# Hybrid attention and recurrence block: when the first recurrent half's heads are turned for the output projection, and which instruction the third weight's casts stand behind at a border

## The chip, the cores and the metric

The kernel runs on one core of a Trainium2 chip. Its time is device microseconds of one execution; the figure for a kernel is the median of its runs. One execution was also recorded by the hardware profiler. TensorE (PE) does matmuls and transposes, VectorE (DVE) and ScalarE (ACT) do elementwise work and empty PE's output banks, GpSimd (POOL) and SyncE (SP) issue most of the transfers. Each engine has its own queue and works through it in order.

## The reference, cut to what matters

One layer, 512 tokens, width 2048, all in float32:

```python
h = rms_norm(x, norm1_w) * (1 + scale1) + shift1      # shift, scale, gate: silu(c) @ w_ada + b_ada
aq, ak, av, gq, gf, gi, gg = split(h @ w_in)          # 7 groups of 1024 columns
attn = rms_norm(dilated_attention(rope(norm(aq)), rope(norm(ak)), av))   # 8 heads of 128
ho = hgrn2(gq, gf, gi, lb)                            # 8 heads of 128, causal gated recurrence
hg = rms_norm(ho) * silu(gg)                          # the norm is over each head's 128
x = x + gate1 * (concat([attn, hg]) @ w_out)
x = x + gate2 * (square(relu(h2 @ w_ff1)) @ w_ff2)    # h2: second norm of x with scale2, shift2
```

## The kernel before

Every float32 matmul is three: an operand is split in a rounded part (hi) and the rest (lo), and PE adds hi*hi, hi*lo and lo*hi in one bank (L205 to L207 where the tokens are on the partitions, L213 to L215 where the channels are). ACT makes a rounded part by a cast, DVE the rest by a subtraction: L39 and L40 for a weight (whi, wlo), L246 and L247 for an operand of 128 channels x 512 tokens (hi, lo).

**Projections.** `project` computes 512 columns from the 16 channel blocks k = 0 to 15 into four banks named prj; a weight here is the 128x512 piece for one k, and two of them come with one load (wraw). One weight costs PE 12 matmuls, three for each bank. The projections with this form come in the order: input of the recurrence (gi), attention's aq, ak, av, all for the first half of the heads; then gq, gi, aq, ak, av for the second half; then the gate hg_gate of the first half and of the second. Behind these comes the output projection in four quarters (`project_out`), which has the same form and takes as operands the 16 turned and scaled head blocks (mix): four heads of the first recurrent half, eight of attention, four of the second recurrent half, in that order. All use the same four banks, so the first weight of a projection can only go into a bank that the copies behind the projection before have emptied: L414 in `evac` (gi, av, and by a helper of qk also aq and ak), L572 in `hgrn_q` (gq), L716 in `hg_gate` (gg). "Border" means the place between two projections.

**Background work on PE.** Attention and recurrence are generators in a list, `tasks`. Behind each weight's matmuls `project` calls `tick`, which takes the first generator one `yield` further, so between two weights stands a step of attention or recurrence. In the first output quarter `tick` goes two steps for each of the first ten weights, and more steps are taken there as long as the next operand has not been turned. The PE order is exactly that in which the Python code issues. ACT, DVE and POOL have their instructions ordered by a scheduler's own estimate of times, in which `tc.high_priority()` and `tc.issue_after(x)` (not ahead of instruction x) are what the code can say.

**Casts at a border.** `load_w(..., cast_behind=True)` ties the two casts of a load, and their low parts, behind the instruction that the list `evacuated` holds, if it holds one. `project` asks for it at its third and fourth weight (k0 == 2), and so does the first output quarter. Before the change only `hg_gate` writes to `evacuated`, at each of its four copies, so the list holds its last bank copy: the tie is there at the border between the two gate projections and at the one into the output projection.

**The recurrent half's output.** `hrs` holds each head's norm factors, `gs` the gate of silu form as four token tiles. `hg_out` multiplies, for each of its four heads, the head's output by norm factor and gate, four DVE instructions in place in gs (L731), yields, and turns the head: `to_mix`, four transposes into one bank (L555, ptm) and ACT's scaled copy into mix (L557). It is preceded in `tasks` by attention's norm and followed by `attention_out`, which turns attention's heads one per step. While the second gate projection runs, `split_early` splits turned heads (L246, L247) that exist by k >= 8; what has not been split then is split in the first output quarter. Of the recurrence itself the prediction names these: `forget` (L564, DVE), levels of the chunk product, for which DVE makes an operand z (L611, L612) and the running products Sx, f (L618, L619), the masks (L656, L659), PE's cross products of level 128 (L673, pD), and the weighted sums L132 (acc) of `gemv`, DVE work for the conditioning vectors that runs beside them.

Of the kernel before, what the change touches and what calls it, by code (L numbers as in the profile page):

```python
# [22 lines left out]
DH = 128  # L23
# [21 lines left out]
def hybrid_block(ctx, tc, x, c, positions, norm1_w, w_ada, b_ada, w_in, q_norm_w, k_norm_w,  # L45
# [3 lines left out]
    pe, dve, act, pool = nc.tensor, nc.vector, nc.scalar, nc.gpsimd  # L49
# [18 lines left out]
    def bank(name, tag="bg"):  # L68
        return ps.tile([P, 512], F32, name=name, tag=tag)
# [30 lines left out]
    n2c, aoc, hgc, posc = cols[:, 0:16], cols[:, 16:24], cols[:, 40:41], cols[:, 44:48]  # L100
# [88 lines left out]
    evacuated = []  # L189
# [45 lines left out]
    def slot(name, dt=F32):  # L235
        return io.tile([P, 512], dt, name=name, tag="io")
# [44 lines left out]
    for q in range(4):  # L281
# [5 lines left out]
        for j in range(4):  # L287
# [3 lines left out]
            t = slot("xnT")  # L291
# [71 lines left out]
    def tick(n=1):  # L363

        for _ in range(n):
            while tasks:
                try:
                    next(tasks[0])
                    break
                except StopIteration:  # L370
                    tasks.pop(0)
# [3 lines left out]
    def project(c0, mm, rate=1.85, after=None):  # L375

        banks = [bank("prj", tag="mm") for _ in range(4)]
        for k0 in range(0, NK, 2):
            for j, (whi, wlo) in enumerate(load_w(win_v, k0, c0, 512, None, behind=len(marks) > 2, cast_behind=k0 == 2)):
                k = k0 + j  # L380
                mm(banks, hhi[k], hlo[k], whi, wlo, k == 0, k == NK - 1)
                tick()
                owed[0] += rate
                while owed[0] >= 1.0:
                    bg_step()
                    owed[0] -= 1.0
                if after:
                    after(k)
            marks.append(asked[0])
        return banks  # L390
# [18 lines left out]
    def evac(banks, name):  # L409
        ts = []  # L410
        for ti in range(NT):
            t = slot(name)
            with tc.high_priority():
                act.copy(t, banks[ti])  # L414
            ts.append(t)
        return ts

# [28 lines left out]
    def qk(c0, name, i):  # L446
        ts = evac(project(c0, tok_mm), name)
        rs = sm.tile([P, NT, 4], F32, name=f"rs{i}", bufs=2)
        bgw.insert(0, qk_norm(ts, i, rs))
        return ts if i else (ts, rs)  # L450
# [101 lines left out]
    def to_mix(k, src, hs, wcol):  # L552
        pt = bank("ptm")
        for ti in range(NT):
            pe.transpose(pt[:, ti * P:(ti + 1) * P], src[ti][:, hs], ident)  # L555
        mix[k] = slot("mix")
        act.activation(mix[k], pt, AF.Identity, scale=wcol)  # L557
# [8 lines left out]
    def hgrn_q(ht):  # L566
        qb = project(3072 + ht * 512, ch_mm)
        qs = []
        for h in range(4):
            q = slot("gq")  # L570
            with tc.high_priority():
                act.copy(q, qb[h])  # L572
            qs.append(q)
        for q in qs:
            sg = wk.tile([P, 512], F32, name="sg", tag="ev", bufs=2)
            act.activation(sg, q, AF.Tanh, scale=0.5)
            dve.tensor_scalar(sg, sg, 0.5 * QS, 0.5 * QS, op0=ALU.mult, op1=ALU.add)
            dve.tensor_tensor(q, q, sg, op=ALU.mult)
        return qs
# [130 lines left out]
    def hg_gate(ht):  # L710
        gb = project(6144 + ht * 512, tok_mm, after=split_early if ht else None)
        gs = []
        for ti in range(NT):
            g = slot("gg")
            with tc.high_priority():
                evacuated[:] = [act.copy(g, gb[ti])]  # L716
            gs.append(g)
        for g in gs:
            sg = wk.tile([P, 512], F32, name="sg", tag="ev", bufs=2)
            act.activation(sg, g, AF.Tanh, scale=0.5)  # L720
            dve.tensor_scalar(sg, sg, 0.5, 0.5, op0=ALU.mult, op1=ALU.add)
            dve.tensor_tensor(g, g, sg, op=ALU.mult)
        return gs

    def hg_out(ht, gs, os_, rs):
        for _ in range(3):
            yield
        for h in range(4):
            hs = slice(h * DH, (h + 1) * DH)
            for ti in range(NT):  # L730
                dve.scalar_tensor_tensor(gs[ti][:, hs], os_[h][:, ti * P:(ti + 1) * P], rs[:, h, ti:ti + 1],  # L731
                                         gs[ti][:, hs], op0=ALU.mult, op1=ALU.mult)
            yield
            to_mix(8 + ht * 4 + h, gs, hs, hgc)

    for b in range(4):
        bgw.append(shift_gen(b))
# [125 lines left out]
    v0 = evac(project(2048, tok_mm), "av")  # L863
    tasks.append(attention(q0, k0_, v0))
    hq1 = hgrn_q(1)
    hv1 = evac(project(5120 + 512, tok_mm), "gi")
    tasks.append(hgrn(f1, hq1, hv1, hrs[1]))
# [4 lines left out]
    gs = hg_gate(0)  # L872
    tasks.append(attention_norm((q0[0], q1[0])))
    tasks.append(hg_out(0, gs, f0, hrs[0]))
    tasks.append(attention_out((q0[0], q1[0])))
    gs = hg_gate(1)
    tasks.append(hg_out(1, gs, f1, hrs[1]))
    while bgw:
        bg_step()


    def project_out(q, rate, after):
        banks = [bank("prj", tag="bg" if q % 2 and i < 2 else "mm") for i in range(4)]
        for i0 in range(0, NK, 2):
            for j, (whi, wlo) in enumerate(load_w(wout_v, korder[i0], q * 512, cast_behind=q == 0 and i0 == 2)):
                i = i0 + j
                while q == 0 and len(mixp) <= i:
                    if not split_mix():
                        tick()
                while q == 0 and split_mix():  # L890
                    pass
                tok_mm(banks, *mixp[i], whi, wlo, i == 0, i == NK - 1)
                tick(2 if q == 0 and i < 10 else 1)
                owed[0] += rate
                while owed[0] >= 1.0:
                    bg_step()
                    owed[0] -= 1.0
                after(i)
        return banks
# [4 lines left out]
    banks = project_out(0, 0, nothing)  # L904
# [52 lines left out]
    for q in range(4):  # L957
        xin = []
        for ti in range(NT):
            t = xr.tile([P, 512], F32, name="xin", tag="x")  # L960
            act.dma_start(t, x_t[:, ti, q * 512:(q + 1) * 512])
            xin.append(t)
        if q:
            banks = project_out(q, 1.7, u_split if q == 3 else nothing)
# [223 lines left out]
    def product(i, src, c, ws, tag, by_tile, nxt):  # L1188


        banks = [bank("f2", tag=tag) for _ in range(2)]
        fh, fl = operand(src, c, i)
        ahead = []

        def mm(u, whi, wlo, ts_):
            for a in range(2):
                for t in ts_:
                    ts = slice(t * P, (t + 1) * P)
                    first, end = u + a == 0, u + a == KG
                    pe.matmul(banks[t], lhsT=fh[u][a][:, ts], rhs=whi[:, a], start=first, stop=False)  # L1200
                    pe.matmul(banks[t], lhsT=fh[u][a][:, ts], rhs=wlo[:, a], start=False, stop=False)  # L1201
                    pe.matmul(banks[t], lhsT=fl[u][a][:, ts], rhs=whi[:, a], start=False, stop=end)  # L1202

        if by_tile:
            for t in range(2):
                for u in range(KG):
                    mm(u, *ws[u], (t,))
        else:
            for u in range(KG):
                mm(u, *ws[u], range(2))  # L1210
                if u == KG - 1 or src is hparts:
                    tick()
                if nxt and u < KG - 1:
                    ahead.append(nxt(u))
        return banks, ahead
# [8 lines left out]
    def turn(b, n, cs):  # L1224

        fs = pools["fs2"].tile([P, FORMS, 2, 256], F32, name="fs2")
        for j in (0, 2, 1, 3):
            pt = bank("pt3")
            for ti in range(NT):
                pe.transpose(pt[:, ti * P:(ti + 1) * P], cs[((5, 7), (6, 1))[ti // 2][1 - n]][ti % 2][:, j * P:(j + 1) * P],  # L1230
                             ident)
            act.activation(block(fs, j), halves(pt), AF.Relu)
            if j >= 2:
                v = fs[:, (j - 2) * 2:(j - 2) * 2 + 2]
                act.activation(v, v, AF.Square)
        yield
        yield from make_forms(fs, fparts, 2 * b + n, stage, True, loads if 2 * b + n == NG - 2 else None)
# [21 lines left out]
    def turned(*a):  # L1259
        tasks.append(turn(*a))  # L1260
        while len(tasks) > 1:
            tick()
        tick()
# [82 lines left out]
    for item, following in zip(items, items[1:] + [None]):  # L1346
# [14 lines left out]
        if stage_ == 1:  # L1361
            banks, ahead = product(i, hparts, 0, ws, "bg" if first and j < 2 else "mm", False, call)
# [10 lines left out]
        else:  # L1373
            q, c = blk
            banks, ahead = product(i, fparts, c, ws, "mm", i == 2 and c == NC - 1, call)
# [68 lines left out]
```

## Time and profile before

| | us |
|---|---|
| median of three runs | 2265.33 |
| lowest, highest | 2263.37, 2268.85 |
| the profiled execution, its own time | 2268.35 |
| its span on the core | 2266.6 |
| PE busy in the span | 2211.3 (98%) |
| DVE busy | 1807.2 (80%) |
| ACT busy | 1098.2 (48%) |

The span is the time between first and last record on the core; the execution's own time has what lies around it as well. A row of the timeline gives the start in us from the span's beginning, the busy time, engine, line, operation, the tile that is written and the tiles that are read, shapes, and how many instructions stand in a row (x4); where the engine was idle ahead of the row, brackets give for how long and which instruction released it. A row of the table of stretches gives its window and length, then busy us and instructions of PE, PE's weight loads, DVE, ACT and POOL, the granted clock, the busy share of the DMA engines and GB/s. Matmul ends are modelled, so starts are the better guide on PE. In the list of waits an entry has the sum, the count and the longest.

### The profile page before, as it was taken

To read this page: it belongs to the slowest core of one execution; us is meant where nothing else is said; L and a number is where in the kernel's file an instruction comes from. 1 tells how busy PE (TensorE), PEld (TensorE's weight loads), DVE (VectorE), ACT (ScalarE), POOL (GpSimd) and SP (SyncE) were. 2 spreads that over 40 slices of the span, in tenths; PEclk is the share of its full clock that TensorE was granted. 3 is DMA by queue.
4 is the path that set the end of the run, shared out by engine and by line. 5 is a ranking of instruction groups with operands and counts; after the bars stand their busy time and mean duration, and the time that the engine had idled before them with its cause. 6 is when DMAs were issued, how large, how long until landed. Compare 5 with 4: busy or idle time off the path is not lost.

```text
span 2266.6 us, 33052 instructions
## 1 busy us (share of the span) xinstructions
PE 2211.3 (98%) x11769; PEld 1827.6 (81%) x11769; DVE 1807.2 (80%) x2765; ACT 1098.2 (48%) x1950; POOL 439.5 (19%) x664
## 2 busy tenths in 40 slices
PE   4899999999999999999999999999999999999999
PEld 3788888888888778888887888888888888888887
DVE  6998988678977457778658988988897779967878
ACT  5555444434444454457544565565564333443332
POOL 1000022001210000003232323332232222222221
PEclk9999999999999999999999999999999999999999
DMA  9797655556564248847879789889979987998884
GB/s 327 252 330 260 214 178 167 178 177 205 174 204 145 76 134 280 273 121 263 324 278 350 285 311 387 302 302 364 336 284 372 364 313 260 349 347 312 300 298 166
DMA packets 262581, 598.30 MB, mean 264 GB/s; under 512 B 23220, under 2 KB 43968, under 8 KB 262416
## 3 DMA queue, kind: packets, MB, share of 16 engines
q1 hardware_dynamic: 186800, 332.54, 43.0%
q0 software_dynamic: 70720, 254.21, 30.6%
q10 hardware_dynamic: 4896, 9.44, 1.3%
q8 instruction: 93, 1.52, 0.3%
q14 instruction: 72, 0.59, 0.1%
HBM read 518.49 MB, written 77.61 MB: 263 GB/s over the span
## 4 chain that ended last, share of the span: by engine, by line
PE 73%; issue 10%; DMA 7%; DVE 5%; POOL 3%; ACT 1%; SPq 0%; POOLq 0%; DVEq 0%; ACTq 0%
PE f L1202 9%; PE f L1200 9%; PE f L1201 9%; PE prj L205 9%; PE prj L207 9%; PE prj L206 9%; PE f L215 2%; PE f L213 2%; PE f L214 2%; DMA Fl<-f_lod 2%; PE prj L214 2%; PE prj L215 2%; PE prj L213 2%; DMA Fl<-h_lod 1%; POOL Fl L1146 1%
## 5 line engine op out<-in xcount | busy, mean ns | idle before, releaser
L1184 ACT CAST vhi<-raw 128x1024 fp32r<-128x1024 f32 x392 | 413.3, 1055 | 520.2 <-PE f L1202 418.4
L1185 DVE TENSOR_TENSOR vlo<-raw,vhi 128x1024 fp32r<-128x1024 f32 x392 | 474.6, 1218 | 140.9 <-ACT vhi L1184 140.5
L1202 PE MATMUL f<-vhi,Fl 128*128 128x512 f32 x1376 | 535.6, 389 | 0.8 <-DMA Fl<-f_lod 0.8
L1201 PE MATMUL f<-vlo,Fh 128*128 128x512 f32 x1376 | 535.8, 389 | 0.5 <-DVE vlo L1185 0.4
L1200 PE MATMUL f<-vhi,Fh 128*128 128x512 f32 x1376 | 536.0, 390 | 0.0
L39 ACT CAST whi<-wraw 128x512 fp32r<-128x512 f32 (+1 forms) x368 | 220.4, 602 | 448.1 <-PE prj L207 297.4
L40 DVE TENSOR_TENSOR wlo<-wraw,whi 128x512 fp32r<-128x512 f32 (+1 forms) x368 | 244.2, 666 | 181.1 <-ACT whi L39 171.0
L205 PE MATMUL prj<-whi,hi 128*128 128x512 f32 x896 | 360.4, 402 | 6.4 <-ACT hi L246 5.8
L207 PE MATMUL prj<-whi,lo 128*128 128x512 f32 x896 | 351.1, 392 | 2.0 <-DVE lo L247 2.0
L206 PE MATMUL prj<-wlo,hi 128*128 128x512 f32 x896 | 350.1, 391 | 0.0
L1201 PEld LDWEIGHTS f<-vlo,Fh 128*128 128x128 f32 x1376 | 258.3, 188 | 55.3 <-DVE vlo L1185 2.0
L1202 PEld LDWEIGHTS f<-vhi,Fl 128*128 128x128 f32 x1376 | 258.3, 188 | 54.9 <-DMA Fl<-f_lod 1.2
L1200 PEld LDWEIGHTS f<-vhi,Fh 128*128 128x128 f32 x1376 | 258.3, 188 | 53.5
L1168 DVE TENSOR_TENSOR raw<-raw,raw 128x1024 f32<-128x1024 f32 x224 | 269.6, 1216 | 4.6 <-DMA raw<-in_w_ff_dram 4.2
L132 DVE SCALAR_TENSOR_TENSOR acc<-araw,sc,acc 128x512 f32<-128x512 f32 (+1 forms) x392 | 250.2, 672 | 24.6 <-DMA araw<-in_w_ada_dram 24.0
L205 PEld LDWEIGHTS prj<-whi,hi 128*128 128x128 f32 x896 | 168.8, 188 | 41.3 <-ACT hi L246 6.3
L207 PEld LDWEIGHTS prj<-whi,lo 128*128 128x128 f32 x896 | 168.8, 188 | 39.2 <-DVE lo L247 2.9
L206 PEld LDWEIGHTS prj<-wlo,hi 128*128 128x128 f32 x896 | 169.1, 189 | 32.9
L1146 POOL DMA_DIRECT2D Fh<-f_hid x112 | 79.0, 705 | 425.8 <-PE f L1202 411.0
L215 PE MATMUL f<-hi,wlo 128*128 128x512 f32 x256 | 99.9, 390 | 1.6 <-DVE wlo L40 1.6
L213 PE MATMUL f<-hi,whi 128*128 128x512 f32 x256 | 100.3, 392 | 0.0
L214 PE MATMUL f<-lo,whi 128*128 128x512 f32 x256 | 99.6, 389 | 0.0
(311 smaller groups left out, 2905.1 us busy)
## 6 DMA issues: line engine op xcount, KB each, us to landing
raw<-in_w_ff_dram SPq DMA_DIRECT2D x224, 512.0 KB, 10.5
araw<-in_w_ada_dram SPq DMA_DIRECT2D x384, 256.0 KB, 4.7
Fh<-f_hid POOLq DMA_DIRECT2D x112, 512.0 KB, 6.5
Fl<-f_lod POOLq DMA_DIRECT2D x112, 512.0 KB, 7.8
wraw<-in_w_in_dram SPq DMA_DIRECT2D x104, 512.0 KB, 4.8
Fh<-h_hid POOLq DMA_DIRECT2D x60, 512.0 KB, 6.5
Fl<-h_lod POOLq DMA_DIRECT2D x60, 512.0 KB, 6.9
f_hid<-part POOLq DMA_DIRECT2D x48, 512.0 KB, 7.6
```

The lines of the kernel that those rows point to most:

```text
L39: nc.scalar.copy(hi, src)
L40: _split.low = (eng or nc.vector).tensor_tensor(lo, src, hi.bitcast(F32), op=ALU.subtract)
L132: dve.scalar_tensor_tensor(acc, raw[:, k - k0], vec[:, k:k + 1], acc, op0=ALU.mult, op1=ALU.add)
L205: pe.matmul(banks[ti], lhsT=hi[:, ts], rhs=whi, start=first, stop=False)
L206: pe.matmul(banks[ti], lhsT=hi[:, ts], rhs=wlo, start=False, stop=False)
L207: pe.matmul(banks[ti], lhsT=lo[:, ts], rhs=whi, start=False, stop=last)
L1168: dve.tensor_tensor(dst, a, b, op=ALU.subtract)
L1184: cast_done.append(act.copy(hi, src))
L1185: split_done.append(dve.tensor_tensor(lo, src, hi.bitcast(F32), op=ALU.subtract))
L1200: pe.matmul(banks[t], lhsT=fh[u][a][:, ts], rhs=whi[:, a], start=first, stop=False)
L1201: pe.matmul(banks[t], lhsT=fh[u][a][:, ts], rhs=wlo[:, a], start=False, stop=False)
L1202: pe.matmul(banks[t], lhsT=fl[u][a][:, ts], rhs=whi[:, a], start=False, stop=end)
```

## The change

The change has two parts. First, `evac` and `hgrn_q` write their bank copies to `evacuated` as `hg_gate` does, so at every border behind such a projection the third and fourth weights' casts stand behind the last bank copy of the projection before. Second, `hg_out` of the first half takes another sequence of steps: two yields ahead of it in place of three; heads 0 and 1 are normalised in one step; the next turns both and normalises head 2; the next normalises head 3; heads 2 and 3 are turned in the two after that. The second half's sequence stays as it was.

```diff
--- before.py
+++ after.py
@@ -411,7 +411,7 @@
         for ti in range(NT):
             t = slot(name)
             with tc.high_priority():
-                act.copy(t, banks[ti])
+                evacuated[:] = [act.copy(t, banks[ti])]
             ts.append(t)
         return ts
 
@@ -569,7 +569,7 @@
         for h in range(4):
             q = slot("gq")
             with tc.high_priority():
-                act.copy(q, qb[h])
+                evacuated[:] = [act.copy(q, qb[h])]
             qs.append(q)
         for q in qs:
             sg = wk.tile([P, 512], F32, name="sg", tag="ev", bufs=2)
@@ -723,15 +723,32 @@
         return gs
 
     def hg_out(ht, gs, os_, rs):
-        for _ in range(3):
-            yield
-        for h in range(4):
+        def normed(h):
             hs = slice(h * DH, (h + 1) * DH)
             for ti in range(NT):
                 dve.scalar_tensor_tensor(gs[ti][:, hs], os_[h][:, ti * P:(ti + 1) * P], rs[:, h, ti:ti + 1],
                                          gs[ti][:, hs], op0=ALU.mult, op1=ALU.mult)
+
+        def turned(h):
+            to_mix(8 + ht * 4 + h, gs, slice(h * DH, (h + 1) * DH), hgc)
+
+        for _ in range(2 + ht):
             yield
-            to_mix(8 + ht * 4 + h, gs, hs, hgc)
+        if ht == 0:
+            for n_, t_ in (((0, 1), ()), ((2,), (0, 1)), ((3,), ())):
+                for h in t_:
+                    turned(h)
+                for h in n_:
+                    normed(h)
+                yield
+            turned(2)
+            yield
+            turned(3)
+        else:
+            for h in range(4):
+                normed(h)
+                yield
+                turned(h)
 
     for b in range(4):
         bgw.append(shift_gen(b))
```

Three places show what moves. The first is PE at the border between the second gate projection (banks prj_8267 to 8270) and the first output quarter. Before, from the last matmul of the gate's last weight (k = 15):

```order
L207 MATMUL prj_8270<-whi_8670,lo15_1194 128x512
L555 MATMUL ptm_8702<-ident_69,gg_8243 128x128
L555 MATMUL ptm_8702<-ident_69,gg_8245 128x128
L555 MATMUL ptm_8702<-ident_69,gg_8247 128x128
L555 MATMUL ptm_8702<-ident_69,gg_8249 128x128
L205 MATMUL prj_8741<-whi_8747,hi0_8713 128x512
L206 MATMUL prj_8741<-wlo_8748,hi0_8713 128x512
L207 MATMUL prj_8741<-whi_8747,lo0_8714 128x512
```

After, from the last matmul of the gate's weight k = 14; what is left out are the other transposes and the rest of the matmuls of weight 15:

```order
L207 MATMUL prj_8270<-whi_8674,lo14_1189 128x512
L555 MATMUL ptm_8694<-ident_69,gg_8243 128x128
...
L555 MATMUL ptm_8694<-ident_69,gg_8249 128x128
L555 MATMUL ptm_8701<-ident_69,gg_8243 128x128
...
L555 MATMUL ptm_8701<-ident_69,gg_8249 128x128
L205 MATMUL prj_8267<-whi_8678,hi15_1193 128x512
...
L207 MATMUL prj_8270<-whi_8678,lo15_1194 128x512
L205 MATMUL prj_8760<-whi_8766,hi0_8712 128x512
L206 MATMUL prj_8760<-wlo_8767,hi0_8712 128x512
L207 MATMUL prj_8760<-whi_8766,lo0_8713 128x512
```

Head 0 was turned between the gate's last matmul and the first output matmul (prj_8741, operand hi0_8713); now heads 0 and 1 are turned (ptm_8694 and ptm_8701) ahead of the gate's last weight, and nothing stands between the gate's last matmul and the first output matmul (prj_8760, operand hi0_8712).

The second is ACT at the same place. Before:

```order
L557 ACTIVATE mix_8707<-ptm_8702,cols_97 128x512
L716 COPY gg_8717<-prj_8267 128x512
L716 COPY gg_8719<-prj_8268 128x512
L716 COPY gg_8721<-prj_8269 128x512
L716 COPY gg_8723<-prj_8270 128x512
L39 CAST whi_8832<-wraw_8830 128x512
L39 CAST whi_8836<-wraw_8830 128x512
L246 CAST hi0_8713<-mix_8707 128x512
L720 ACTIVATE sg_8725<-gg_8717 128x512
L720 ACTIVATE sg_8729<-gg_8719 128x512
```

After:

```order
L557 ACTIVATE mix_8699<-ptm_8694,cols_97 128x512
L557 ACTIVATE mix_8706<-ptm_8701,cols_97 128x512
L246 CAST hi0_8712<-mix_8699 128x512
L716 COPY gg_8736<-prj_8267 128x512
L246 CAST hi1_8732<-mix_8706 128x512
L716 COPY gg_8738<-prj_8268 128x512
L720 ACTIVATE sg_8744<-gg_8736 128x512
L716 COPY gg_8740<-prj_8269 128x512
L716 COPY gg_8742<-prj_8270 128x512
L39 CAST whi_8847<-wraw_8845 128x512
L39 CAST whi_8851<-wraw_8845 128x512
L720 ACTIVATE sg_8748<-gg_8738 128x512
```

The head's copy into mix had the four bank copies (gg) and two weight casts behind it, and then came the operand's cast hi0. Now two heads' copies come first, the casts hi0 and hi1 go in front of and between the bank copies, one tanh (L720) goes between them, and the two weight casts come behind the fourth.

The third is DVE in the first recurrent head, at the operand z_2939 of level 128, behind the mask's sum (near_2550), at about 268 us of the span. Before:

```order
L656 TENSOR_TENSOR near_2550<-near_2550,mt_2931 128x128
L564 TENSOR_SCALAR f_2087<-f_2087,omlb_1314,lb_1313 128x512
L612 TENSOR_TENSOR z_2939<-gq_1300,f_1292 128x2x128
L618 TENSOR_TENSOR Sx_2549<-Sx_2549,f_1292 128x2x128
L564 TENSOR_SCALAR f_2089<-f_2089,omlb_1314,lb_1313 128x512
L132 SCALAR_TENSOR_TENSOR acc_2945<-araw_2990,sc_86,acc_2945 128x512
L659 TENSOR_TENSOR AT0_457<-near_2550,mt_2931 32x4x32 x4
L132 SCALAR_TENSOR_TENSOR acc_2944<-araw_3037,sc_86,acc_2944 128x512
L564 TENSOR_SCALAR f_2091<-f_2091,omlb_1314,lb_1313 128x512
L564 TENSOR_SCALAR f_2093<-f_2093,omlb_1314,lb_1313 128x512
```

After:

```order
L656 TENSOR_TENSOR near_2550<-near_2550,mt_2931 128x128
L619 TENSOR_TENSOR f_1292<-f_1292 128x4x64
L611 TENSOR_TENSOR z_2939<-kk_2547,Sx_2549 128x2x128
L564 TENSOR_SCALAR f_2089<-f_2089,omlb_1314,lb_1313 128x512
L132 SCALAR_TENSOR_TENSOR acc_2945<-araw_2990,sc_86,acc_2945 128x512
L132 SCALAR_TENSOR_TENSOR acc_2944<-araw_3037,sc_86,acc_2944 128x512
L564 TENSOR_SCALAR f_2091<-f_2091,omlb_1314,lb_1313 128x512
L659 TENSOR_TENSOR AT0_457<-near_2550,mt_2931 32x4x32 x4
L612 TENSOR_TENSOR z_2939<-gq_1300,f_1292 128x2x128
L564 TENSOR_SCALAR f_2093<-f_2093,omlb_1314,lb_1313 128x512
L618 TENSOR_TENSOR Sx_2549<-Sx_2549,f_1292 128x2x128
```

The second half of the operand (L612) stood two behind the mask's sum; now the products f and the first half of the operand, two L564, two L132 and the four mask additions of L659 stand between them. In the second half's first head a weight's low part (L40) goes ahead of the same instruction.

## The prediction

> **What bounds the kernel now.** I first read the page's busy times, then the waits of PE, then one table of stages.
>
> ```profile
> span 2266.6 us, 33052 instructions
> PE 2211.3 (98%) x11769; PEld 1827.6 (81%) x11769; DVE 1807.2 (80%) x2765; ACT 1098.2 (48%) x1950; POOL 439.5 (19%) x664
> ...
> PE prj L205 <- ACT hi L246: 5.8, 2, 4.3
> ...
> 190.00:786.78 596.78, 596.20 (x4494) 493.26 (x4493) 463.54 (x1033) 266.89 (x766) 64.64 (x110) 1.00 0.55 179
> 786.78:806.95 20.17, 12.35 (x49) 9.29 (x48) 12.34 (x31) 10.66 (x20) 0.00 (x0) 0.83 0.24 78
> 806.95:1000.00 193.05, 192.50 (x901) 159.35 (x900) 127.68 (x204) 91.47 (x195) 8.76 (x16) 1.00 0.65 214
> 1000.00:2266.00 1266.00, 1257.54 (x5640) 1041.50 (x5638) 1044.09 (x1123) 622.87 (x727) 351.16 (x505) 1.00 0.85 310
> ```
>
> PE is the bound: from 190 us to 786.78 it is idle for 0.58 us in all, from 806.95 to 1000 for 0.55 us. Between those stands the one bad place after the start, 20.17 us in which PE is idle for 7.8 us and its granted clock is 0.83. That is the border from the second gate projection to the first quarter of the output projection. ACT's cast L246, which ends 5.8 us of waits in two places, a longest of 4.3, belongs there too. PE, in its own timeline:
>
> ```profile
> 784.06 0.39 PE L205 MATMUL prj<-whi,hi 128*128 128x512 f32 x1
> ...
> 786.78 0.60 PE L555 MATMUL ptm<-ident,gg 128*128 128x128 f32 x4
> 791.66 0.50 PE L205 MATMUL prj<-whi,hi 128*128 128x512 f32 x1 [4.27 <-ACT hi L246]
> ...
> 799.08 0.50 PE L205 MATMUL prj<-whi,hi 128*128 128x512 f32 x1 [1.51 <-ACT hi L246]
> ...
> 801.70 0.50 PE L207 MATMUL prj<-whi,lo 128*128 128x512 f32 x1 [1.89 <-DVE lo L247]
> ...
> 806.95 0.47 PE L205 MATMUL prj<-whi,hi 128*128 128x512 f32 x1
> ...
> 809.80 1.03 PE L555 MATMUL ptm<-ident,aq 128*128 128x128 f32 x8
> 810.59 0.48 PE L205 MATMUL prj<-whi,hi 128*128 128x512 f32 x1
> ...
> 814.21 0.47 PE L205 MATMUL prj<-whi,hi 128*128 128x512 f32 x1
> ```
>
> At 784.06 the gate's last weight begins; its 12 matmuls end at 786.78. Then head 0 is turned, and the first output matmul needs that head's copy, cast and low part. ACT shows why this takes 4.27 us:
>
> ```profile
> 787.42 0.69 ACT L557 ACTIVATE mix<-ptm,cols 128x512 f32<-128x512 f32 x1 [5.26 <-PE ptm L555]
> 788.01 2.04 ACT L716 COPY gg<-prj 128x512 f32<-128x512 f32 x4
> 789.91 1.18 ACT L39 CAST whi<-wraw 128x512 fp32r<-128x512 f32 x2
> 790.95 0.66 ACT L246 CAST hi<-mix 128x512 fp32r<-128x512 f32 x1
> 791.47 1.19 ACT L720 ACTIVATE sg<-gg 128x512 f32<-128x512 f32 x2
> ```
>
> ACT was idle for 5.26 us, since the head's copy stands first in its queue; then four bank copies and two weight casts go between the head's copy and its cast. The clock makes it dearer:
>
> ```profile
> 789.34:792.75 3.41, 0.93 (x3) 1.00 0.01 2
> 792.75:796.16 3.41, 3.41 (x9) 0.50 0.49 154
> 796.16:799.58 3.42, 1.91 (x13) 1.00 0.03 7
> 799.58:802.99 3.41, 1.52 (x7) 1.00 0.87 290
> 802.99:806.40 3.41, 3.41 (x13) 0.50 0.03 11
> ```
>
> Two stretches of 3.41 us ran at half the granted clock, each behind a stretch in which PE was busy for 0.93 or 1.52 us; the one with 1.91 busy had none behind it. A half-clock stretch full of matmuls loses half its length, 1.7 us.
>
> **The change, part by part.** The sum is made against the profiled execution: span 2266.6, its own time 2268.35, which is 3.02 above the median of 2265.33.
>
> First, the border. From 786.78 to 806.95 PE issues 24 transposes and 24 matmuls. At full pace 12 matmuls and 8 transposes take 814.21 - 810.59 = 3.62 us and 8 transposes 810.59 - 809.80 = 0.79, so this work needs 2 x 3.62 + 0.79 = 8.03 us. The border costs 20.17 - 8.03 = **12.1 us**: 7.7 in the three waits, 3.4 in two half-clock stretches, 1.0 in pipeline starts. No instruction is added or removed; transposes, copies, casts and DMAs only move.
>
> What is left of it, with today's durations: heads 0 and 1 are turned at 784.06 (0.79), so the last weight runs from 784.85 to 787.57, and the first output weight needs banks 0 to 3 at 787.57, 788.25, 788.93 and 789.61. A head's copy starts 0.64 after its transposes begin, as now (786.78, 787.42): 784.70. By the rows above ACT advances 0.59 for a head's copy, 0.52 for its cast, 1.90/4 = 0.48 for a bank copy and 0.60 for a tanh. In the new order the bank copies start at 786.40, 787.40, 788.47 and 788.95, and end some 0.55 later. Banks 0 and 1 are free in time, bank 2 about 0.15 late, bank 3 in time. Head 0's cast ends at 786.5, a microsecond early; the wait of 4.27 has nothing left to wait for. The normalised heads that are turned sooner have long been done (the first row below, at 743.06, holds the last four of sixteen).
>
> The next risk is DVE, which has to make the third pair's low part (the wait of 1.89 today, moved on). Its durations:
>
> ```profile
> 743.06 1.13 DVE L731 SCALAR_TENSOR_TENSOR gg<-f,hrs,gg 128x128 f32<-128x128 f32 x4
> ...
> 792.41 0.75 DVE L721 TENSOR_SCALAR sg<-sg 128x512 f32<-128x512 f32 x2
> 793.08 1.28 DVE L722 TENSOR_TENSOR gg<-gg,sg 128x512 f32<-128x512 f32 x2
> ...
> 798.26 0.68 DVE L40 TENSOR_TENSOR wlo<-wraw,whi 128x512 fp32r<-128x512 f32 x1
> 798.87 2.18 DVE L731 SCALAR_TENSOR_TENSOR gg<-f,hrs,gg 128x128 f32<-128x128 f32 x8
> ```
>
> From the first tanh's end (788.5) there stand ahead of it three L721 (0.34 each), three L722 (0.61), three weights' low parts (0.61) and eight L731 (0.26): 6.8 us, so it ends at 788.5 + 6.8 + 0.68 = 796.0. PE wants it at 787.57 + 0.15 + 2.72 + 1.19 (12 transposes) + 2.72 + 0.79 + 0.46 = 795.6: a wait of 0.35. The border keeps **0.5 us**. From below its cost is nothing; from above both waits reach 1.9, and half-clock stretches follow, some 4 us. I take 0.5, since it is added up from rows in the queue's order. Gain: 12.1 - 0.5 = 11.6.
>
> Second, the casts at the other nine borders. The third weight's cast moves behind the last bank copy. Cover: PE still has two weights' matmuls to do, 5.4 us. The tightest of them, before the second value projection, by DVE and PE:
>
> ```profile
> 621.16 0.81 DVE L40 TENSOR_TENSOR wlo<-wraw,whi 128x512 fp32r<-128x512 f32 x1
> ...
> 624.05 0.39 PE L206 MATMUL prj<-wlo,hi 128*128 128x512 f32 x1
> ```
>
> The third weight's low part now takes the slot in which the fourth's stands (621.16 to 621.97); its first user is at 624.05. It stays 2.1 us early: no cost, and a loss only if ACT or DVE ran that much later. Nor is there a gain, PE being idle there for under 0.6 us in all.
>
> But DVE's order changes with it, and twice PE's cross product of level 128 comes to wait:
>
> ```profile
> 267.36 0.41 DVE L612 TENSOR_TENSOR z<-gq,f 128x256 f32<-128x256 f32 x1
> ...
> 268.03 0.54 DVE L564 TENSOR_SCALAR f<-f,omlb,lb 128x512 f32<-128x512 f32 x1
> 268.49 0.74 DVE L132 SCALAR_TENSOR_TENSOR acc<-araw,sc,acc 128x512 f32<-128x512 f32 x1
> 269.15 1.17 DVE L659 TENSOR_TENSOR AT<-near,mt 32x128 f32<-32x128 f32 x4
> ...
> 270.94 0.71 PE L673 MATMUL pD<-z 128*128 128x128 f32 x4
> ...
> 578.78 0.42 DVE L612 TENSOR_TENSOR z<-gq,f 128x256 f32<-128x256 f32 x1
> ...
> 579.36 0.71 PE L673 MATMUL pD<-z 128*128 128x128 f32 x4
> ```
>
> In the first head two L132 (0.66 each), two L564 (0.46) and four L659 (1.20 together) go ahead of the product's operand: 3.4 us later, ready at 267.36 + 3.4 + 0.41 = 271.2 where PE is at 270.94, a wait of 0.25. In the second half's first head a weight's low part (0.61) goes ahead of it: ready at 579.8 for 579.36, 0.45. Together **0.7 us** lost; from below nothing, from above 1.5, if each is half a microsecond worse. Later reorderings of one or two instructions around 1242 us have more room than they move.
>
> Sum: 11.6 - 0.7 = 10.9 us. The profiled execution would take 2257.5; the median 2265.33 - 10.9 = **2254.4 us**. Nothing downstream should take it back: PE keeps its pace to the end (1257.54 of 1266.00 busy from 1000 us on), so no load is late there by more than a part of 8.5 us.
>
> **Rivals.** *The border keeps a large wait.* Bank copies share ACT with two head copies, two casts and a tanh, and low parts wait behind eight L731. If either comes 1.5 us later than added up, PE has a gap of about 1.9 us, as at 801.70, and a half-clock stretch behind it: 3.6 us kept, 2258.0. For it: ACT's order interleaves them. Against: the sums have ACT's last copy 0.1 us early.
>
> *Another bound takes over.* If loads set the pace of the last 1266 us (DMA share 0.85), the gain becomes a wait for them: 2265.3. Against: PE is idle for only 8.5 us there.
>
> [...]
>
> *Slower.* The casts come late at the nine other borders, in ACT's and DVE's queues behind bank copies that themselves wait for PE. From 2.1 us later on, PE waits; were each wait 1.8 us with a half-clock stretch behind it, that is 9 x 3.5 = 31.5, so 2254.4 + 31.5 = 2285.9. An average of 1.2 us a border already eats the gain. Against: the fourth weight's cast stands there today and has its microseconds of room.
>
> **How the numbers follow.** Forecast 0.66, large wait kept 0.14, clock stretch stays 0.05, another bound 0.10, slower 0.05. The range: the sum's bounds are 12.1 + 0.6 (the small waits elsewhere too) and 12.1 - 4 - 1.5 = 6.6, so 2252.6 to 2258.7; the runs before spread from 2263.37 to 2268.85, so I go 3 us below and 2 above: 2249.5 to 2261. A measurement of this kernel can tell 0.3% from no change, 6.8 us: faster means below 2258.5. That holds for nearly all of the forecast and the clock case and half of the kept wait: 0.77. Within 0.3%: the rest of these and the other bound, 0.18. Slower: 0.05.
>
> **What would show it.** Right: PE's wait for ACT's cast at L246 gone from the list, no half-clock stretch around 793 or 803, the third output weight starting some 11 us sooner; waits of a few tenths at L673 (pD) near 271 and 579. Wrong: a wait of PE for a gg copy or a low part of over 1.5 us behind the gate, PE waiting for weights' low parts at other borders, or DMA waits after 1000 us that add up to several microseconds.

## The result

| | median, us | runs | ratio to the kernel before, 95% interval |
|---|---|---|---|
| before | 2265.53 (2263.37 to 2268.85) | 5 | |
| the change | 2256.49 (2254.72 to 2259.68) | 5 | 0.9961 (0.9947 to 0.9975) |

The change makes the kernel 9.0 us faster. Forecast were 2254.4 us and a range of 2249.5 to 2261. The profiled execution of the change took 2254.72 us, 13.6 less than that of before; this pair overstates the change, as the stages below show.

The table of stages of the changed kernel, as it was read for the kernel before. The second row runs from the end of the gate's next to last weight (k = 14) to the place from which PE's order is the same in both kernels again:

```profile
190.00:785.25 595.25, 592.69 (x4478) 490.39 (x4477) 462.65 (x1033) 265.10 (x763) 65.67 (x110) 1.00 0.55 178
785.25:819.85 34.60, 34.46 (x181) 28.57 (x180) 23.98 (x49) 26.59 (x48) 0.00 (x0) 1.00 0.35 112
990.00:2252.00 1262.00, 1255.35 (x5638) 1040.04 (x5636) 1044.04 (x1122) 621.98 (x726) 351.13 (x505) 1.00 0.85 310
```

At the border PE is now idle for 0.14 us of 34.60, at the full clock (1.00 in the row). In the first row it is idle for 2.56 us, where it was idle for 0.58 before. PE's waits name the place:

```profile
PE pD L673 <- DVE z L612: 2.0, 2, 1.0
...
PE prj L205 <- ACT aq L414: 0.5, 1, 0.5
```

The entries for ACT's cast L246 and DVE's low part L247 are gone; an entry for the cross product of level 128 is new. PE at the border of the changed kernel:

```profile
785.25 1.04 PE L555 MATMUL ptm<-ident,gg 128*128 128x128 f32 x8
786.04 0.48 PE L205 MATMUL prj<-whi,hi 128*128 128x512 f32 x1
...
788.86 0.39 PE L205 MATMUL prj<-whi,hi 128*128 128x512 f32 x1
...
790.22 0.50 PE L205 MATMUL prj<-whi,hi 128*128 128x512 f32 x1
790.55 0.40 PE L206 MATMUL prj<-wlo,hi 128*128 128x512 f32 x1
...
796.90 0.40 PE L206 MATMUL prj<-wlo,hi 128*128 128x512 f32 x1
797.44 0.51 PE L207 MATMUL prj<-whi,lo 128*128 128x512 f32 x1
...
820.21 0.48 PE L205 MATMUL prj<-whi,hi 128*128 128x512 f32 x1
```

The gate's last weight runs from 786.04, and the first output weight follows at 788.86 with nothing between. Two traces of a wait are left. Between 796.90 and 797.44 L207 waits for the third operand's low part, which DVE ends at 797.38 (begun at 796.69, 0.69 us). At 790.22 the third bank is taken just behind its copy, which ends at 790.16, and the next matmul follows after 0.33 in place of the usual 0.23. ACT beside it:

```profile
785.89 1.26 ACT L557 ACTIVATE mix<-ptm,cols 128x512 f32<-128x512 f32 x2 [2.55 <-PE ptm L555]
787.05 0.62 ACT L246 CAST hi<-mix 128x512 fp32r<-128x512 f32 x1
787.55 0.60 ACT L716 COPY gg<-prj 128x512 f32<-128x512 f32 x1
788.03 0.64 ACT L246 CAST hi<-mix 128x512 fp32r<-128x512 f32 x1
788.55 0.61 ACT L716 COPY gg<-prj 128x512 f32<-128x512 f32 x1
789.03 0.66 ACT L720 ACTIVATE sg<-gg 128x512 f32<-128x512 f32 x1
789.56 1.09 ACT L716 COPY gg<-prj 128x512 f32<-128x512 f32 x2
```

The first operand's cast ends at 787.67, 1.2 us before PE wants it, and the bank copies start at 787.55, 788.55, 789.56 and some 0.5 later.

The same stages, worked out from the starts of the same PE instructions in each profile, show what belongs to the change. "Middle" runs from the 1201st PE instruction of the trace (a matmul of the first recurrent head, near 264 us) to the start of the gate's weight k = 14; "border" from the end of that weight to the L205 that stands at 820.21 above (830.55 before); "FFN entry" (the end of the output projection and the beginning of the feed-forward network) is the 1500 PE instructions from 970 us (before) on, with the transposes near 1230 us. The experiments below are in the table already:

| profile | start of middle | middle | border | FFN entry |
|---|---|---|---|---|
| before | 263.74 | 517.60 | 46.50 | 340.18 |
| before, second | 261.87 | 517.99 | 46.26 | 337.09 |
| tie alone | 262.84 | 519.95 | 44.05 | 336.57 |
| the change | 262.82 | 519.71 | 34.96 | 336.74 |
| the change, second | 263.04 | 519.71 | 34.98 | 339.37 |
| heads alone | 263.94 | 517.97 | 34.94 | 337.19 |
| heads alone, second | 263.18 | 517.59 | 34.98 | 342.04 |
| change, masks tied | 264.09 | 519.23 | 34.98 | 338.33 |
| head 0 alone sooner | 262.09 | 517.95 | 36.94 | 337.05 |
| pair at the border | 263.64 | 517.91 | 40.83 | 336.36 |

The border gains 11.5 us (11.3 between the second profiles) and the middle loses 2.1 us in the first pair of profiles. The start and the FFN entry differ by up to 2.2 and 5.7 us between profiles whatever the kernel; of the 13.6 us between the first two profiled executions, 0.9 and 3.4 come from these two and are not the change's.

### The profile page after: what moved, and what is told of

It reads as the page before. It is cut to its first block, busy times and chain, and to the rows that moved or that the text cites. A ratio compares the mean times of both kernels' runs of the same rounds, so it can differ in the third digit from the quotient of the medians.

```text
span 2252.8 us, 33043 instructions
## 1 busy us (share of the span) xinstructions
PE 2205.3 (98%) x11769; PEld 1823.7 (81%) x11769; DVE 1807.0 (80%) x2765; ACT 1096.5 (49%) x1950; POOL 440.5 (20%) x664
## 3 DMA queue, kind: packets, MB, share of 16 engines
q8 instruction: 93, 1.52, 0.3%
## 4 chain that ended last, share of the span: by engine, by line
PE 79%; DVE 7%; issue 6%; DMA 6%; POOL 1%; ACT 1%; SPq 0%; POOLq 0%; DVEq 0%; ACTq 0%
PE f L1219 12%; PE f L1217 12%; PE f L1218 12%; PE prj L205 8%; PE prj L207 8%; PE prj L206 8%; PE f L215 2%; PE f L214 2%; PE f L213 2%; PE prj L213 2%; PE prj L214 2%; PE prj L215 2%; DMA f_lod<-fs 1%; DMA Fl<-f_lod 1%; DVE acc L132 1%
## 5 line engine op out<-in xcount | busy, mean ns | idle before, releaser
L40 DVE TENSOR_TENSOR wlo<-wraw,whi 128x512 fp32r<-128x512 f32 (+1 forms) x368 | 245.5, 672 | 165.1 <-ACT whi L39 157.3
L205 PE MATMUL prj<-whi,hi 128*128 128x512 f32 x896 | 360.0, 402 | 0.6 <-ACT aq L414 0.5
L207 PE MATMUL prj<-whi,lo 128*128 128x512 f32 x896 | 350.3, 391 | 0.1
L132 DVE SCALAR_TENSOR_TENSOR acc<-araw,sc,acc 128x512 f32<-128x512 f32 (+1 forms) x392 | 251.0, 677 | 24.3 <-DMA araw<-in_w_ada_dram 23.8
L207 PEld LDWEIGHTS prj<-whi,lo 128*128 128x128 f32 x896 | 168.2, 188 | 36.7 <-DVE lo L247 0.6
L205 PEld LDWEIGHTS prj<-whi,hi 128*128 128x128 f32 x896 | 168.4, 188 | 35.1 <-ACT ak L414 0.9
```

The lines of the kernel that those rows point to most:

```text
L40: _split.low = (eng or nc.vector).tensor_tensor(lo, src, hi.bitcast(F32), op=ALU.subtract)
L132: dve.scalar_tensor_tensor(acc, raw[:, k - k0], vec[:, k:k + 1], acc, op0=ALU.mult, op1=ALU.add)
L205: pe.matmul(banks[ti], lhsT=hi[:, ts], rhs=whi, start=first, stop=False)
L207: pe.matmul(banks[ti], lhsT=lo[:, ts], rhs=whi, start=False, stop=last)
```

## The experiments

### The second part alone: heads turned sooner, the tie left where it was

```diff
-                evacuated[:] = [act.copy(t, banks[ti])]
+                act.copy(t, banks[ti])
...
-                evacuated[:] = [act.copy(q, qb[h])]
+                act.copy(q, qb[h])
```

> The second part alone: the first recurrent half's heads 0 and 1 turned together one step sooner, none at the border; the tie behind bank copies stays only where it was (the two borders behind gate projections). Theory: the border's whole gain (11.5 us in the profile of the changed kernel) comes from this part, and the two waits of PE at the cross product of level 128 (1.03 and 0.96 us, a net 0.15 and 1.03 against before) come from the other part, through DVE's order. Then the border stays without a wait of PE, both waits are under 0.1 us, and the median is 2256.49 - 1.2 = 2255.3 us. Rival: the tie at all borders has a share in the border's gain; then a wait of 2 us or more is back between the gate and the output projection, 2259 us or more.

Median 2253.86 us, ratio 0.9949 (0.9937 to 0.9961). The table of stages of this kernel has the border as short as with the whole change, and the stage before it idle for 0.5 us:

```profile
190.00:784.64 594.64, 594.12 (x4483) 491.11 (x4482) 463.48 (x1033) 266.97 (x767) 64.68 (x110) 1.00 0.55 179
784.64:819.23 34.59, 34.45 (x181) 28.56 (x180) 23.97 (x49) 26.60 (x48) 0.00 (x0) 1.00 0.35 112
```

Neither of the two waits at level 128 is there. So the border's gain comes from the heads alone, and the tie at the other nine borders adds nothing to it. The median is 1.4 us under the one expected, which is less than these executions differ among themselves (2253.08 to 2260.43).

### The first part alone: the tie at all borders, heads as before

```diff
-                act.copy(t, banks[ti])
+                evacuated[:] = [act.copy(t, banks[ti])]
...
-                act.copy(q, qb[h])
+                evacuated[:] = [act.copy(q, qb[h])]
```

> The first part alone: the third weight's casts tied behind the last bank copy at all borders, the heads turned as before. Theory: the border takes 20.2 us as before (three waits of PE near 4.3, 1.5 and 1.9 us), the wait at level 128 near 580 us is there with about 1.0 us, the one near 271 us with 0.1 to 1.1 us as far as PE comes there earlier or later, no other border changes; median 2265.53 + 1.2 = 2266.7 us. Rival: the tie is worth something at the borders, 2263 us or less. Rival: the waits at level 128 were an accident of that execution, 2265.5 us.

Median 2266.0 us, ratio 0.9997 (0.9989 to 1.0006). PE's waits in this kernel hold both the old and the new ones:

```profile
PE prj L205 <- ACT hi L246: 5.8, 2, 4.3
PE pD L673 <- DVE z L612: 2.0, 2, 1.0
```

No other border changed: against the kernel before, the places at 271 and 580 us are the only ones in the middle at which PE loses more than 0.25 us, 1.07 and 0.97. The middle takes 519.95 us, 2.1 more than the mean of the six profiles without the tie (517.84). The time as a whole does not show this. The border took 44.05 in this execution for 46.50 and 46.26 in the two of before: its three waits add up to 6.33 us for 7.67 and 6.77, and its half-clock stretches hold 5.41 us of PE's busy time for 6.82 and 9.27, of which half is taken as lost, 2.7 for 3.4 and 4.6 (in the first half-clock stretch of the kernel before, matmuls start 0.43 us apart, for 0.23 outside it). By time alone the tie would pass for neutral; the two waits are in all of the three profiles that have the tie and DVE's order as the change has it, with 0.93 to 1.03 us each, and in none of the six without the tie.

### Head 0 alone sooner, head 1 at the border

```diff
-            for n_, t_ in (((0, 1), ()), ((2,), (0, 1)), ((3,), ())):
+            for n_, t_ in (((0, 1), ()), ((2,), (0,)), ((3,), (1,))):
```

This and the next one are built on the second part alone.

> As the second part alone, but only head 0 is turned a step sooner; head 1 is turned at the border. Theory: what counts is which instruction stands at the head of ACT's queue when the banks are full. Head 0's cast is in time, so the wait of 4.3 us is gone, but head 1's copy stands ahead of the four bank copies and waits for its transposes at the border: the first bank copy ends 0.64 + 0.59 + 0.55 = 1.8 us after the gate's last matmul, where PE wants the bank after 0.4 us of transposes: one wait of about 1.4 us for a bank copy (gg), no half-clock stretch; median 2255.3 + 1.5 = 2256.8 us. Rival (the pair is what counts, the second operand is late without it): a wait of 1.5 us for the second operand's cast or low part as well, with half-clock stretches, 2260 us.

Median 2256.88 us, ratio 0.9954 (0.9941 to 0.9967). PE and ACT of this kernel:

```profile
785.98 0.60 PE L555 MATMUL ptm<-ident,gg 128*128 128x128 f32 x4
787.83 0.50 PE L205 MATMUL prj<-whi,hi 128*128 128x512 f32 x1 [1.25 <-ACT gg L716]
...
796.92 0.50 PE L207 MATMUL prj<-whi,lo 128*128 128x512 f32 x1 [0.66 <-DVE lo L247]
```

```profile
786.62 0.69 ACT L557 ACTIVATE mix<-ptm,cols 128x512 f32<-128x512 f32 x1 [1.87 <-PE ptm L555]
787.20 2.04 ACT L716 COPY gg<-prj 128x512 f32<-128x512 f32 x4
```

ACT idles for 1.87 us with full banks behind it, because head 1's copy stands first in its queue and its transposes stand behind the gate's last matmul. PE then waits 1.25 us for the first bank, close to the 1.4 expected. A wait of 0.66 us for the third operand's low part (796.92) comes on top that was not expected; what makes it longer than with both heads turned is not shown. The second operand is in time without being one of a pair, against the rival. The border takes 36.94, 2.0 more than with both turned.

### Both heads turned together, but at the border

```diff
-            for n_, t_ in (((0, 1), ()), ((2,), (0, 1)), ((3,), ())):
+            for n_, t_ in (((0, 1), ()), ((2,), ()), ((3,), (0, 1))):
```

> As the second part alone, but heads 0 and 1 are turned together at the border, as late as head 0 was. Theory: turning sooner is what removes the large wait: the first output matmul waits for head 0's cast, which stands behind two head copies, four bank copies and two weight casts, 4.6 us, with one half-clock stretch of 3.41 us behind it (1.7 us lost); the second operand is in time, so the wait of 1.5 us is gone. About 7 us of the border's cost stay: 2262.5 us. Rival (turning the pair together is enough): 2256 us.

Median 2260.15 us, ratio 0.9974 (0.9963 to 0.9984). PE's timeline and two stretches of this kernel:

```profile
787.00 1.04 PE L555 MATMUL ptm<-ident,gg 128*128 128x128 f32 x8
792.44 0.57 PE L205 MATMUL prj<-whi,hi 128*128 128x512 f32 x1 [4.41 <-ACT hi L246]
```

```profile
789.31:792.72 3.41, 0.28 (x1) 0.28 (x2) 1.33 (x3) 3.41 (x8) 0.00 (x0) 1.00 0.00 0
792.72:796.14 3.42, 3.42 (x9) 2.24 (x9) 3.42 (x8) 2.13 (x5) 0.00 (x0) 0.50 0.50 156
```

The large wait is back with 4.41 us and one half-clock stretch behind it, 3.42 us at a clock of 0.50, of which half, 1.7, is put as lost; 4.4 + 1.7 = 6.1 answers to 40.83 - 34.96 = 5.9 us. The second and the third wait of the kernel before are not there. Turning sooner is what removes the large wait, as expected, but 5.9 us stay where some 7 were expected, and the median is 2.35 us lower than forecast. So turning the pair together, with the heads normalised sooner for it, is worth 46.50 - 40.83 = 5.7 us of the 11.5 (5.4 from the second profile of before), and turning it a step sooner, which removes the large wait with its stretch, the other 5.9.

### The change with the masks tied behind level 128's operand

```diff
-        for r in range(4):
-            rr = slice(r * 32, r * 32 + 32)
-            dve.tensor_tensor(AT[rr, 0:4, rr], near[rr], mt[rr, 1], op=ALU.add)
         z128 = level(128)
+        with tc.issue_after(level_last[0].ins):
+            for r in range(4):
+                rr = slice(r * 32, r * 32 + 32)
+                dve.tensor_tensor(AT[rr, 0:4, rr], near[rr], mt[rr, 1], op=ALU.add)
```

(`level_last` holds the instruction L612 of the level issued last. In this kernel's rows L612 has the number L613, L673 is L675 and the masks' L659 is L662.)

> The change as it is, and in each recurrent head the four mask additions (AT, 1.17 us together) are tied behind the second half of level 128's operand on DVE; the tie of the casts at all borders stays. Theory: the two waits of PE at level 128 are only a matter of what stands ahead of the operand on DVE. With 1.17 us less ahead of it, the first wait (1.03 us) is gone; at the second the operand comes 1.17 - 0.39 (one weighted sum's start now ahead of it) = 0.8 us sooner, and of 0.96 us some 0.2 stay. The border stays free of waits. Median 1 to 1.9 us under the change's, 2255 us. Rival: the operand is late for another reason (its factors come late from ACT or from loads), then both waits stay near 1 us and the median at 2256.5 us.

Median 2256.87 us, ratio 0.9955 (0.9941 to 0.9970): nothing gained over the change in time, and 0.5 us in the middle (519.23 for 519.71). PE waits in the first head, and nothing at the second place; PE and DVE of this kernel:

```profile
271.28 0.71 PE L675 MATMUL pD<-z 128*128 128x128 f32 x4
...
278.78 1.10 PE L687 MATMUL pE<-z 128*128 128x256 f32 x4 [1.33 <-DVE z L613]
```

```profile
270.61 0.42 DVE L613 TENSOR_TENSOR z<-gq,f 128x256 f32<-128x256 f32 x1
270.95 0.27 DVE L662 TENSOR_TENSOR AT<-near,mt 32x128 f32<-32x128 f32 x1
...
277.62 0.68 DVE L40 TENSOR_TENSOR wlo<-wraw,whi 128x512 fp32r<-128x512 f32 x1
278.22 0.42 DVE L613 TENSOR_TENSOR z<-gq,f 128x256 f32<-128x256 f32 x1
```

Both waits at level 128 are gone, so they were a matter of what stands ahead of the operand on DVE. But in the first head a wait of 1.33 us for the operand of level 256 (278.22) is new. From level 128's operand to this one it is 7.61 us where it is 5.67 in the change (270.54 to 276.21): the four mask additions, 1.17 us, now stand between the two, and so does a weight's low part (L40, some 0.6), which comes behind the second one in the change. What was put behind one operand stands in front of the next. The expectation was right on the cause and wrong on the gain.

### The heads alone, the change and the kernel before once more

Three unaltered kernels, for a direct comparison and second profiles.

> The second part alone once more, beside the whole change on one chip. Theory: 1.2 us (first part's waits: net 0.15 and 1.03) to 2.1 us faster than the whole change. Rival: the two are the same, and the 2.6 us between their medians was scatter. A second profile also shows whether the waits at level 128 stay away.

> The whole change once more, unaltered, for the comparison with the second part alone. Expected: 2256.5 us as before; in its second profile the same waits of about 1 us at level 128, the border without a wait, and a start that may take 1 us more or less.

> The kernel before, unaltered, for a second profile. The first shows a wait of 1.82 us at 1235 us with a half-clock stretch behind it, 2.9 us that the change's profile lacks. If these belong to the kernel before, they are here again; if they are this one execution's, the wait is 0.6 us as in the other profiles and no stretch follows, and the span is some 3 us shorter. The border takes about 20 us in both cases.

Medians 2255.89 (ratio 0.9953, 0.9939 to 0.9967), 2256.51 (0.9954, 0.9941 to 0.9966) and 2268.07 us (1.0005, 0.9995 to 1.0015). The heads alone are faster than the whole change by 2.6 us in the first comparison and 0.6 in this one, with overlapping intervals: the times do not settle that difference. The profiles do for the stage: the middle takes 517.59 to 517.97 us in the two profiles of the heads alone and 519.71 in the two of the whole change, so by this stage the first part of the change costs some 2 us and earns nothing. Much of the scatter comes from one place near 1230 us, here in PE's timelines of the change, of the heads alone and of the kernel before, second profiles each (in kernels with the new `hg_out`, line numbers behind it are 17 higher, so L1247 is the L1230 of before):

```profile
1226.02 0.44 PE L1247 MATMUL pt<-ident,s 128*128 128x128 f32 x2 [2.00 <-DVE s L1266]
```

```profile
1226.73 0.44 PE L1247 MATMUL pt<-ident,s 128*128 128x128 f32 x2 [2.01 <-DVE s L1266]
```

```profile
1232.17 0.44 PE L1230 MATMUL pt<-ident,s 128*128 128x128 f32 x2 [0.59 <-DVE s L1249]
```

The same wait was 0.60 us in the first profile of the change, 0.83 in that of the heads alone and 1.82 in that of before. Its length belongs to the execution, not to the kernel.

## Why the prediction was right, and where a size was off

**The border.** Right in mechanism and in size. Expected were 12.1 us of cost, of which 0.5 stay; the border gained 46.50 - 34.96 = 11.5. The wait for the first operand's cast has nothing left to wait for, the bank copies start a little earlier than added up (786.36 for 786.40 and 788.37 for 788.47, when 1.19 us are taken off for the later start of the stage), and the two small waits left are those forecast: 0.10 at the third bank for 0.15, and for the third pair's low part 797.44 - 796.90, which is 0.31 longer than the usual step of 0.23, for 0.35. No half-clock stretch is left (granted clock 1.00 over the 34.60 us). The 1.0 us of the cost that was put down to pipeline starts was the remainder of a sum; the rows of before show 0.3 of it, since the first matmul behind each of the three waits has 0.33 or 0.34 us to the next (791.66 to 791.99) for the usual 0.23.

**The casts at the other nine borders.** Right: no new wait there, and no gain. The one wait for a copy that the list of the change still holds (L414, 0.5 us, near 288 us) is in all ten profiles, those of before included. The tie alone shows the same without the other part.

**The two waits at level 128.** Right in place and cause; the size is the term that was off. The step gave "a wait of 0.25" and "0.45. Together 0.7 us"; PE lost 1.08 us at the first (its lead of 0.93 over the kernel before becomes a lag of 0.15) and 1.03 at the second, 2.1 in all. DVE of the kernel before and of the change, a little earlier than the rows on which the step rested, shows what was missed at the first:

```profile
263.24 0.42 DVE L612 TENSOR_TENSOR z<-gq,f 128x256 f32<-128x256 f32 x1
263.57 0.42 DVE L618 TENSOR_TENSOR Sx<-Sx,f 128x256 f32<-128x256 f32 x1
263.97 0.69 DVE L40 TENSOR_TENSOR wlo<-wraw,whi 128x512 fp32r<-128x512 f32 x1
```

```profile
263.04 0.69 DVE L40 TENSOR_TENSOR wlo<-wraw,whi 128x512 fp32r<-128x512 f32 x1
...
264.31 0.42 DVE L612 TENSOR_TENSOR z<-gq,f 128x256 f32<-128x256 f32 x1
...
265.05 0.42 DVE L618 TENSOR_TENSOR Sx<-Sx,f 128x256 f32<-128x256 f32 x1
...
270.54 0.42 DVE L612 TENSOR_TENSOR z<-gq,f 128x256 f32<-128x256 f32 x1
```

Two instructions of level 64, L612 and L618, stood ahead of a weight's low part (L40) and now stand behind it. From that L40 to the operand it is 7.50 us where it was 3.39 (263.97 to 267.36), 4.1 more, not the 3.4 of the step: the two instructions of 0.33 each were not counted, because the piece of the order that was compared began at L656. With them the step would have given 0.9, and PE starts 0.15 us behind the operand's end (271.11 for 270.96), which the step left out as well: 1.06 of the 1.08. At the second place the weight's low part was counted, but DVE came to the head about half a microsecond later already (the weighted sum L132 ahead of it started at 573.53 for 572.78, with PE only 0.2 later); with it 0.45 becomes 1.0. Why DVE was behind there is not shown.

**The sum.** 11.5 - 2.1 = 9.4 us answers to the 9.0 between the medians. The measured median is 2.1 us above the forecast, inside its range: 1.4 of it is the 0.7 that should have been 2.1, and the rest is less than the start and the FFN entry, on which the forecast put nothing, differ between executions. With executions that differ by several microseconds, 9.4 against 9.0 is a closer agreement than the times can vouch for.

**The rivals.** A large wait kept at the border, and another bound downstream, did not come: the stretch from 990 us on has PE idle for 6.7 of 1262.00 us. The slower case fell with the first part alone. The case with a chance of 0.05, that a clock stretch stays at the border (2254.4 + 1.7 = 2256.1), fell as well: the stretches at the border stand in profiles with a large wait of PE there (4.27 us in the kernel before, 4.41 with both heads at the border), and with the large waits gone none of the five profiles with both heads turned sooner has one (34.94 to 34.98 us each).

## What to carry to other kernels

Where one engine both empties the banks and prepares the next stage's first operand, the copy of an operand that depends on work issued at the border holds up the bank copies behind it in the queue: here ACT idled ahead of that copy for 5.26 us in the kernel before, and for 1.87 us with head 1 left at the border. Issue that work one step sooner, and all of it, since a head left at the border still cost 2 us here. And when an ordering edit lets a scheduler rearrange another engine, count everything between a common instruction and the reader, not only the rows around the reader.

## What the runs showed of the hardware

In the first profile of the kernel before the half-clock stretches begin at 93.02, 792.75, 802.99 and 1236.48 us; the later three lie 205, 208 and 335 steps of 3.4133 us behind the first, to within 0.01 us. In the first profile of the change they begin at 53.40 and 94.36, 12 such steps apart. With both profiles divided into such steps, from the first record of the clock (35.0 and 32.9 us) to 2245 us, there are seven at the full clock in which PE was busy for at most 1.52 us. Six of them were followed by a half-clock step; the one from 785.92 in the kernel before, with 1.47, was not. Of those with 1.90 us or more (1.91 from 796.16) none was. Of the seven steps at half clock, the one from 93.02, with PE busy for 1.91 us, was followed by a second; the six with 3.11 us or more were not. In the second profile of the kernel before, one with 2.83 us (from 789.59) was followed by a second. Near 1230 us a wait of about 2 us had a half-clock stretch behind it in one execution and none in another. The stretch that holds the transposes near 1230 us, in the second profile of the change and the first of the kernel before:

```profile
1224.75:1228.17 3.42, 1.98 (x16) 1.75 (x17) 3.42 (x5) 1.18 (x3) 0.00 (x0) 1.00 1.06 388
1228.17:1231.58 3.41, 3.41 (x17) 2.81 (x17) 1.18 (x3) 3.38 (x5) 0.00 (x0) 1.00 0.87 285
```

```profile
1233.07:1236.48 3.41, 1.43 (x11) 0.84 (x10) 3.41 (x6) 1.32 (x2) 0.00 (x0) 1.00 1.06 389
1236.48:1239.90 3.42, 3.42 (x15) 3.03 (x13) 1.64 (x2) 3.19 (x6) 0.00 (x0) 0.50 1.05 385
```

In the first pair of rows, around the wait of 2.00 us, PE was still busy for 1.98 of 3.42 us, and no half-clock stretch came behind it; in the second, around the wait of 1.82 us, it was busy for 1.43 of 3.41, and one came. That the place of a wait between the steps makes this difference is the author's estimate from these rows.
